# Score levels of a linear-attention mixer on two pairs of PSUM banks by turns

## Chip, cores, metric

One core of a Trainium2 chip runs the kernel. The metric is the device time of one execution in microseconds (us); the median of a few runs is compared.

## What is computed

The reference is a block of two layers of a latent generator, over 256 context tokens and 256 latent tokens with 1024 features. The even layer holds a linear-attention group with gates (GLA, 4 heads with 64 key and 128 value features) beside an mLSTM group (4 heads of 128); the odd layer is a state-space mixer. Each layer has a modulated RMSNorm ahead of it and a convolutional SwiGLU network behind it. The change touches only the scores of the GLA group. Cut to what matters, for one direction:

```
cum = jnp.cumsum(lac, axis=1)
rel = jnp.where(tri, cum[:, :, None] - cum[:, None, :], -jnp.inf)
att = jnp.einsum('bthk,bshk,btshk->bhts', qc, kc, jnp.exp(rel))
o = jnp.einsum('bhts,bshv->bthv', att, vc) + jnp.einsum('bthk,bhkv->bthv', qc * jnp.exp(cum), s)
```

The decay differs for every feature, so the score of two tokens is not a product of one matrix with another. Forward and backward scans are added up.

## The kernel before

Activations are feature-major: features on the 128 partitions, the 512 tokens along the free axis. Weights stream in as blocks of 128x128; each is split into a high and a low float32r part (`wh` by ScalarE, L168; `wl` by VectorE or GpSimd, L169), and a projection takes three products per block (L180 to L182 where features come out on partitions, L215 to L217 where tokens do). A projection of one column tile over all tokens is 24 matmuls of 512 columns.

The GLA part runs in `even_mixer`, in a loop over two pairs of heads (`for j in range(2)`); the two heads of a pair lie in the two halves of the partitions (64 each). Scores are computed by levels. A first level, without decays, gives the diagonal. Then level n, for n from 0 to 7, gives the scores between the two halves of each block of 2^(n+1) tokens: q and k are multiplied by exponentials of the cumulative gates relative to the middle of the block (tile `EX` of tag `b4`: four subtractions on VectorE, L623 to L626, an exponential on ScalarE, L627, a product on VectorE, L628), and `scores` multiplies them. In `scores`, each token tile t and head `par` gives one matmul of 64 rows by 128 columns (L597), which the profile shows as two records; a level is 8 matmuls and 16 records, and the lines are called with the two heads by turns. Head 0 writes one PSUM bank, head 1 another. Then VectorE takes each bank into `att` under the mask of the level (L603; L606 for the first level), and for level 7 ScalarE copies it into `off` (L633). The tile with `att` and `off` (tag `ao`) exists once, so head pair 1 can write it when head pair 0's outputs (L672) are through.

PSUM has eight banks: four of tag `g` (`gps`), three of tag `m` (`mps`), one of tag `v` (`vps`). Projections take tag `g`. Scores, transposes and outputs take tag `m`. A tile is asked for where the program calls it, and its bank comes free after the last reader.

In head pair 1, each level n is preceded by one of the eight projections with convolution of the mLSTM queries and keys (`ml_in.pop(0)()`, through `conv_silu`): 24 matmuls into a bank of tag `g`, then an activation on ScalarE (L571) and two taps on VectorE (L336, L337) that read the bank, and two passes more. After level 7 of head pair 1 the mLSTM values are projected (`gemm_t`, L635: four banks of tag `g`, L215 to L217).

The order of instructions is not written out by hand. The Tile scheduler lays the whole program out: each engine gets a fixed list of instructions, made by a priority that follows the program's order among what the scheduler takes to be ready, with the tiles' slots (PSUM banks, SBUF tiles by tag) given out as it goes. Each engine then works through its own list and waits on semaphores.

Of the kernel before, what the change touches and what calls it, by code (L numbers as in the profile page):

```python
# [13 lines left out]
ALU = mybir.AluOpType  # L14
AX = mybir.AxisListType

P = 128
# [6 lines left out]
# causal pieces of a 256-token segment, keys in tile t: (direction, t, queries from, to, mask column, offset)  # L24
# [27 lines left out]
def block_kernel(ctx: ExitStack, tc: tile.TileContext, A: dict, out: bass.AP):  # L52
# [55 lines left out]
    def rsqrt(ss, scale, eps):  # L108
        """(ss * scale + eps) ** -0.5 of a few columns, by Newton steps from the exponent's halving"""
        n = ss.shape[-1]  # L110
        m, y, w = (np_.tile([P, 16], F32, tag=t, name=nm(t), bufs=2)[:, :n] for t in ("rm", "ry", "rw"))
        v.tensor_scalar(out=m, in0=ss, scalar1=scale, scalar2=eps, op0=ALU.mult, op1=ALU.add)
        v.tensor_scalar(out=w.bitcast(I32), in0=m.bitcast(I32), scalar1=1, scalar2=None, op0=ALU.logical_shift_right)
        v.tensor_scalar(out=y.bitcast(I32), in0=w.bitcast(I32), scalar1=-1.0, scalar2=1597463007.0, op0=ALU.mult, op1=ALU.add)
        for _ in range(3):
            v.tensor_tensor(out=w, in0=y, in1=y, op=ALU.mult)
            v.scalar_tensor_tensor(out=w, in0=w, scalar=-0.5, in1=m, op0=ALU.mult, op1=ALU.mult)
            v.scalar_tensor_tensor(out=y, in0=w, scalar=1.5, in1=y, op0=ALU.add, op1=ALU.mult)
        return y

    def colsum(sq, c=0, ps=None):
        """column sums of sq [128, n] with the columns on partitions: [128, n / 128] of a PSUM tile"""
        nt = sq.shape[-1] // P
        ps = vps() if ps is None else ps
        for t in range(nt):
            # each product overwrites all but the first column of the one before
            te.matmul(out=ps[:, c + t:c + t + P], lhsT=sq[:, t * P:(t + 1) * P], rhs=ones[:, :P], start=True, stop=True)
        return ps[:, c:c + nt]

    def spread(col, out):  # L130
        """out[:, t] = col[t % 128, t // 128] on every partition"""
# [7 lines left out]
    class Stream:  # L139
        def __init__(self, src, nblocks, fill=None, every=1, skip=0, ahead=1, pool=rawp, eng=lambda u: v):  # L140
            """fill: other work, one piece of it put ahead of every `every`-th transfer's products;
            ahead: how many splits run ahead of the products; eng: what computes the low parts"""
# [5 lines left out]
        def load(self, d):  # L148
            """transfer d to its place in SBUF"""
            if self.rawi != d:  # L150
                w = min(16, self.n - d * 16) * P
                self.raw = self.pool.tile([P, 2048], F32, tag="raw", name=nm("raw"))
                # the first transfer in halves, its second one with its split
# [30 lines left out]
    def gemm_f(st, b0, nk, acts, c0=0, c1=T, bank=gps, ks=None):  # L184
        """feature-major: [128 columns of W, tokens c0:c1]"""
# [7 lines left out]
    def gemm_k(st, b0, nk, acts, spans, pss=None, ks=None):  # L193
        """as gemm_f for a few column tiles at once (blocks [k][tile]), so that products start with the first k"""
# [12 lines left out]
    def gemm_t(st, b0, nk, acts, tiles):  # L207
        """token-major: [128 tokens, 512 columns of W] per token tile"""
# [21 lines left out]
    def mod_chunk(l, j, pool=rawp, psa=vps, tag="raw", n=2, bufs=None):  # L230
        """512 of the vectors' columns, their weights in n transfers"""
# [11 lines left out]
    def mod_part(q, pool, psa):  # L243
        """as mod_chunk, 256 columns of the first layer's mixer norm"""
# [8 lines left out]
    def mod_out(l, c, n, ps, psa):  # L253
        """add up the quadrants, with the columns on partitions: n tiles of 128 columns from tile c"""
# [10 lines left out]
        if i in (1, 4):  # L265
            # (1 + scale) * gain, in place of scale
            v.scalar_tensor_tensor(out=dst, in0=dst, scalar=1.0, in1=col("nmg" if i == 1 else "nfg", l * 8 + k), op0=ALU.add, op1=ALU.mult)
# [3 lines left out]
    class Norm:  # L271
        """1 / rms over the features of tokens c0:c1, a feature tile at a time"""
# [17 lines left out]
        def cols(self):  # L290
            """[token % 128, token tile]"""
            return rsqrt(self.most, 1.0 / D, EPS)

        def row(self):
            """on all partitions, the tokens along the free axis"""
# [29 lines left out]
    # residual: x += gate * y  # L325
# [6 lines left out]
    def conv_side(y, ps, w0, w2):  # L332
        """the two outer taps of a width-3 convolution within each segment"""
# [12 lines left out]
    def warm(n, rhs):  # L346
        """products of ones, so that the tensor engine keeps its clock up while the first data come"""
# [3 lines left out]
    with tc.tile_pool(name="stp", bufs=6) as stp:  # L351
# [13 lines left out]
        def start(k, acts):  # L365
            # the first products run as their K tiles come, between the parts of shift and scale
# [35 lines left out]
    with ExitStack() as st:  # L402
# [6 lines left out]
        def turn(k):  # L409
            """the gain, then token-major"""  # L410
# [29 lines left out]
def even_mixer(E, st, acts, pss0, then):  # L440
# [52 lines left out]
    # log_sigmoid(x) = min(x, 0) - ln(1 + exp(-|x|)), each table loaded once  # L493
# [60 lines left out]
    # token-major columns: [t, tile, row of RQ], and the end-state weights of the context  # L554
# [30 lines left out]
    for j in range(2):  # L585
# [5 lines left out]
        def scores(Q, K, sink, flip=0):  # L591
            pps = [mps().rearrange("p (a b) -> p a b", b=P) for _ in range(2)]
# [13 lines left out]
        scores(q, k, lambda par, pp: v.scalar_tensor_tensor(out=att[par], in0=pp, scalar=2.0, in1=idb, op0=ALU.mult, op1=ALU.mult))  # L606
        for n in range(8):
# [6 lines left out]
            if n == 0:  # L614
# [3 lines left out]
                scores(EX[:, 0, :], k, masked(0))  # L618
# [11 lines left out]
            if n < 7:  # L630
                scores(Q, K, masked(n))
            else:
                scores(Q, K, lambda par, pp: s.copy(out=off[par], in_=pp), 1)  # L633
# [3 lines left out]
        # end state of the context, both directions  # L637
# [22 lines left out]
        # outputs, token-major, and their norm per head  # L660
# [28 lines left out]
    # q and k carry a factor 2 each from the tanh form of silu  # L689
# [4 lines left out]
    def head(h):  # L694
# [5 lines left out]
        # end state of the context: [k, value | norm] per direction  # L700
# [15 lines left out]
        for sg in range(2):  # L716
# [4 lines left out]
            # [s, t] weights: forward s0 -> t 0:256, s1 -> t 128:256; backward s0 -> t 0:128, s1 -> t 0:256  # L721
# [28 lines left out]
    def finish(h):  # L750
        # output gate (twice it), norm, transposed
# [53 lines left out]
def conv_ffn(E, st, l, acts, fill, then):  # L805
# [20 lines left out]
    def around(y, ps, ti):  # L826
        """the other taps"""
# [15 lines left out]
    # VectorE keeps to one operand from SBUF where GpSimd works beside it  # L843
# [3 lines left out]
    def project(j):  # L847
# [5 lines left out]
        elif not full:  # L853
            # a pair to a bank; the others hold sums of the down-projection
# [3 lines left out]
        else:  # L858
            # the down-projection takes the usual banks before the last two are through
# [9 lines left out]
    for hf in range(nh):  # L869
# [6 lines left out]
        for jj in range(per):  # L876
# [4 lines left out]
            # the down-projection's first columns, as far as their K tiles are there  # L881
# [4 lines left out]
            if jj == per - 2 and not full:  # L886
                # and a column more while the last pairs are convolved
# [25 lines left out]
        if full and last:  # L913
            # the last two a segment at a time, so that the next norm starts on the first
# [6 lines left out]
def odd_mixer(E, st, acts, then):  # L921
# [13 lines left out]
    # dt, B, C, B: the context first, C without it  # L935
# [8 lines left out]
    def conv_silu(b0, ti, out, c0):  # L944
        """out = 2 silu(conv + bias)"""
# [13 lines left out]
    def group(q):  # L959
# [5 lines left out]
        # x and B each carry a factor 2  # L965
# [6 lines left out]
        # [s, dir, 384]: forward s0 x t 0:256, s1 x t 128:256; backward s1 x t 0:256, s0 x t 0:128  # L972
# [12 lines left out]
    # softplus(x) = max(x, 0) + ln(1 + u), u = exp(-|x|), with the rounding of 1 + u put back  # L985
# [24 lines left out]
    # token-major: context w_end = exp(c_end - cum) dt [s, dir*32 + head]; latent cum and dt  # L1010
# [7 lines left out]
    tok = T_([P, 2, P], "tokc")     # [s, tile, cum (64) | dt (64)]  # L1018
# [33 lines left out]
    def tokens(i):  # L1052
        """token-major x: context weighted for the end state, latent by dt, per direction; D x"""
# [4 lines left out]
        xw = T_([P, 2, 2, 2, 64], "xw", pool=sp)    # [s, tile, dir, head, 64]  # L1058
        xd = T_([P, 2, 2, 2, 64], "xd", pool=sp)    # [s, dir, tile, head, 64]
# [13 lines left out]
    def decays(i):  # L1073
        """masked C B^T times the decays between tokens; the cumulative sums (negated) broadcast to all partitions"""
# [3 lines left out]
        G = T_([P, 2, 2, 384], "G", pool=sp)        # [s, dir, head, parts]  # L1078
# [15 lines left out]
    def inter(i):  # L1094
        """from the end states, each direction, times its decay since them"""
# [9 lines left out]
    def outputs(i):  # L1105
# [9 lines left out]
        # times (twice) silu(z), square sum per group  # L1115
# [41 lines left out]
def blocks_f(w, ms):  # L1157
    """feature-major blocks of w (K, M): for each column tile, its K tiles"""
# [3 lines left out]
def blocks_k(w, ms):  # L1162
    """feature-major blocks, for each K tile its column tiles"""
# [3 lines left out]
def blocks_kf(w):  # L1167
    """four column tiles together, then the other four one by one"""
# [3 lines left out]
def blocks_t(w, c0):  # L1172
    """token-major blocks: for each K tile, four column tiles from c0"""
# [11 lines left out]
def cols(vv):  # L1185
    """vector -> [128, n] with feature f at [f % 128, f // 128]"""
# [3 lines left out]
def layout(inp):  # L1190
# [40 lines left out]
    # even in-projection  # L1231
# [19 lines left out]
    # FFN  # L1251
# [11 lines left out]
    # odd in-projection  # L1263
# [12 lines left out]
    # constants of the shapes  # L1276
# [29 lines left out]
```

## Time and profile before

| | |
|---|---|
| runs | 1298.69, 1298.11, 1303.0 us; median 1298.69 |
| span of the profiled execution, first to last instruction | 1300.7 us |
| TensorE (PE) busy | 1245.6 us, 96% |
| VectorE (DVE) busy | 942.7 us, 72% |
| ScalarE (ACT) busy | 597.2 us, 46% |
| GpSimd (POOL) busy | 381.4 us, 29% |
| mean granted clock of TensorE | 0.989 |

The profile gives one execution; of its own time only the span is known, which lies between the second and the third of the runs. Times in rows are counted from the span's start. Busy time is the union of an engine's instructions; matmuls overlap in the array, so their single durations add up to more than it. The clock is a share of full speed: 1.00 is 2.4 GHz and 0.50 is 1.2 GHz.

### The profile page before, as it was taken

The numbers are of one execution on the slowest core, as the hardware profiler recorded it, in microseconds if no ns is written. First come the engines' busy times: TensorE is split into PE (matmuls) and PEld (weight loads), VectorE is DVE, ScalarE is ACT, GpSimd is POOL, SyncE is SP. The second block draws the span as 40 slices with busy tenths as digits, with TensorE's granted clock in tenths as the row PEclk, the third lists the DMA queues.
The fourth block names the chain that finished last, engine by engine and source line by source line (L and its number), as shares of the span: only waits on it lengthen the run. The fifth ranks groups of instructions, "written<-read, shape, count | busy, mean of one in ns | idle before, by whom it ended". The sixth has DMA issues, their size and how long they took to land.

```text
span 1300.7 us, 19329 instructions
## 1 busy us (share of the span) xinstructions
PE 1245.6 (96%) x7358; PEld 1027.8 (79%) x7358; DVE 942.7 (72%) x2137; ACT 597.2 (46%) x947; POOL 381.4 (29%) x214
## 2 busy tenths in 40 slices
PE   7999999999999999999999998999999999899987
PEld 5557787876867777888888897888888888899987
DVE  4483899576659766237774488788888957999993
ACT  3463344343344433124442266565566545555553
POOL 0100000000226646136664000122222124678720
PEclk8999999999999999999999999999999998999999
DMA  9556303324445664232202136444363473545431
GB/s 373 184 190 230 117 12 111 109 89 165 166 175 213 254 232 135 98 123 97 98 33 98 65 106 175 130 153 131 114 152 105 153 251 132 207 164 181 156 130 66
DMA packets 39964, 190.96 MB, mean 147 GB/s; under 512 B 4592, under 2 KB 10552, under 8 KB 20928
## 3 DMA queue, kind: packets, MB, share of 16 engines
q1 hardware_dynamic: 36512, 185.48, 41.3%
q10 hardware_dynamic: 3360, 4.25, 1.1%
q8 instruction: 58, 0.95, 0.3%
q14 instruction: 34, 0.28, 0.1%
HBM read 188.51 MB, written 1.20 MB: 146 GB/s over the span
## 4 chain that ended last, share of the span: by engine, by line
PE 71%; DVE 19%; ACT 3%; issue 3%; DMA 3%; POOL 1%; SPq 0%; ACTq 0%; DVEq 0%; POOLq 0%
PE gps L180 14%; PE gps L181 13%; PE gps L182 13%; DVE y L829 6%; PE mps L180 4%; PE mps L182 4%; PE mps L181 4%; PE vps L239 3%; PE vps L1114 2%; DVE ml L897 2%; DVE y L893 1%; PE gps L215 1%; PE gps L217 1%; PE gps L216 1%; PE vps L1100 1%
## 5 line engine op out<-in xcount | busy, mean ns | idle before, releaser
L169 POOL TENSOR_TENSOR wl<-raw,wh 128x1024 fp32r<-128x1024 f32 x111 | 268.1, 2426 | 515.2 <-ACT wh L168 515.0
L168 ACT ACTIVATE wh<-raw 128x1024 fp32r<-128x1024 f32 x226 | 237.3, 1054 | 173.1 <-PE gps L182 107.3
L180 PE MATMUL gps<-hh,wh 128*128 128x512 f32 (+1 forms) x840 | 297.1, 355 | 7.1 <-ACT hh L316 5.4
L182 PE MATMUL gps<-hl,wh 128*128 128x512 f32 (+1 forms) x840 | 295.6, 354 | 1.6 <-DVE hl L318 1.6
L181 PE MATMUL gps<-hh,wl 128*128 128x512 f32 (+1 forms) x840 | 295.4, 352 | 0.4 <-DVE wl L169 0.3
L829 DVE SCALAR_TENSOR_TENSOR y<-mps,fcw,y 128x255 f32<-128x255 f32 (+3 forms) x576 | 223.0, 426 | 38.7 <-ACT y L823 32.5
L169 DVE TENSOR_TENSOR wl<-raw,wh 128x1024 fp32r<-128x1024 f32 x115 | 140.9, 1232 | 81.1 <-ACT wh L168 80.9
L180 PEld LDWEIGHTS gps<-hh,wh 128*128 128x128 f32 x840 | 159.5, 190 | 43.2 <-issue 12.1
L180 PE MATMUL mps<-hh,wh 128*128 128x256 f32 (+1 forms) x528 | 172.7, 327 | 10.9 <-DVE y L829 8.6
L182 PEld LDWEIGHTS gps<-hl,wh 128*128 128x128 f32 x840 | 160.0, 191 | 25.0 <-issue 4.2
L181 PEld LDWEIGHTS gps<-hh,wl 128*128 128x128 f32 x840 | 160.0, 191 | 23.6 <-issue 4.1
L181 PE MATMUL mps<-hh,wl 128*128 128x256 f32 (+1 forms) x528 | 171.1, 324 | 0.0
L182 PE MATMUL mps<-hl,wh 128*128 128x256 f32 (+1 forms) x528 | 171.1, 324 | 0.0
L180 PEld LDWEIGHTS mps<-hh,wh 128*128 128x128 f32 x528 | 101.0, 191 | 27.8 <-issue 9.3
L180 PE MATMUL gps<-mh,wh 128*128 128x256 f32 (+1 forms) x352 | 117.7, 334 | 2.7 <-ACT mh L896 2.7
L181 PE MATMUL gps<-mh,wl 128*128 128x256 f32 (+1 forms) x352 | 117.2, 333 | 0.0
L182 PE MATMUL gps<-ml,wh 128*128 128x256 f32 (+1 forms) x352 | 117.0, 333 | 0.0
L182 PEld LDWEIGHTS mps<-hl,wh 128*128 128x128 f32 x528 | 101.1, 192 | 7.4
L181 PEld LDWEIGHTS mps<-hh,wl 128*128 128x128 f32 x528 | 101.0, 191 | 7.3
L829 DVE SCALAR_TENSOR_TENSOR y<-gps,fcw,y 128x189 f32<-128x189 f32 (+3 forms) x196 | 83.2, 437 | 23.3 <-ACT y L823 19.4
L823 ACT ACTIVATE y<-mps,fcw 128x256 f32<-128x256 f32 (+1 forms) x66 | 40.6, 639 | 87.7 <-PE mps L182 87.7
L180 PEld LDWEIGHTS gps<-mh,wh 128*128 128x128 f32 x352 | 66.8, 190 | 10.0 <-ACT mh L896 2.9
(281 smaller groups left out, 1850.4 us busy)
## 6 DMA issues: line engine op xcount, KB each, us to landing
raw<-in_up SPq DMA_DIRECT2D x42, 1024.0 KB, 5.0
rawm<-in_modw SPq DMA_DIRECT2D x36, 1024.0 KB, 5.7
raw<-in_win SPq DMA_DIRECT2D x32, 1024.0 KB, 5.4
raw<-in_dn SPq DMA_DIRECT2D x20, 1024.0 KB, 5.0
raw<-in_wout SPq DMA_DIRECT2D x10, 1024.0 KB, 5.1
rawm<-in_mods SPq DMA_DIRECT2D x8, 1024.0 KB, 14.0
R<-crd SPq DMA_DIRECT2D x32, 256.0 KB, 4.5
rawm<-in_modw SPq DMA_DIRECT2D x8, 512.0 KB, 5.3
```

What stands on the lines that cost most here:

```text
L168: s.activation(out=hi[:, :n], in_=rw, func=AF.Copy)
L169: self.eng(u).tensor_tensor(out=lo[:, :n], in0=rw, in1=hi[:, :n].bitcast(F32), op=ALU.subtract)
L180: te.matmul(out=ps, lhsT=lhi, rhs=rhi, start=first, stop=False)
L181: te.matmul(out=ps, lhsT=llo, rhs=rhi, start=False, stop=False)
L182: te.matmul(out=ps, lhsT=lhi, rhs=rlo, start=False, stop=last)
L215: te.matmul(out=ps, lhsT=ah[:, sl], rhs=hi[:, c:c + 512], start=k == 0, stop=False)
L216: te.matmul(out=ps, lhsT=ah[:, sl], rhs=lo[:, c:c + 512], start=False, stop=False)
L239: te.matmul(out=ps[32 * (k % 4):32 * (k % 4) + 32, :], lhsT=spad[:, k, :], rhs=raw[:, kk * 512:(kk + 1) * 512], start=k < 4, stop=k >= 4)
L823: s.activation(out=y, in_=ps, func=AF.Identity, scale=fcw[:, ti * 10 + 4:ti * 10 + 5], bias=fcw[:, ti * 10 + 9:ti * 10 + 10])
L829: v.scalar_tensor_tensor(out=o, in0=i, scalar=fcw[:, ti * 10 + wi:ti * 10 + wi + 1], in1=o, op0=ALU.mult, op1=ALU.add)
L897: part = lambda ya=ya, h_=h_, l_=l_: ep.tensor_tensor(out=l_, in0=ya, in1=h_.bitcast(F32), op=ALU.subtract)
L1114: te.matmul(out=py[r, a:e], lhsT=l, rhs=rr, start=n == 0, stop=n == len(mm) - 1)
```

## The change

`scores` gets the number of the level and takes its two banks from tag `m` for an even number and from tag `g` for an odd one. The first level is called with 1. In a head pair the levels then ask for `g`, `m`, `g`, `m`, and so on, to `g` for level 7. Matmuls, masks and their order in the program stay the same. The rest of the diff takes comments and docstrings out.

```
-        def scores(Q, K, sink, flip=0):
-            pps = [mps().rearrange("p (a b) -> p a b", b=P) for _ in range(2)]
+        def scores(n, Q, K, sink, flip=0):
+
+            pps = [(mps, E.gps)[n % 2]().rearrange("p (a b) -> p a b", b=P) for _ in range(2)]
...
-        scores(q, k, lambda par, pp: v.scalar_tensor_tensor(out=att[par], in0=pp, scalar=2.0, in1=idb, op0=ALU.mult, op1=ALU.mult))
+        scores(1, q, k, lambda par, pp: v.scalar_tensor_tensor(out=att[par], in0=pp, scalar=2.0, in1=idb, op0=ALU.mult, op1=ALU.mult))
...
-                scores(EX[:, 0, :], k, masked(0))
+                scores(0, EX[:, 0, :], k, masked(0))
...
-                scores(Q, K, masked(n))
+                scores(n, Q, K, masked(n))
...
-                scores(Q, K, lambda par, pp: s.copy(out=off[par], in_=pp), 1)
+                scores(n, Q, K, lambda par, pp: s.copy(out=off[par], in_=pp), 1)
```

## Rows read from the trace of the kernel before

**Rows 1.** The page, part 1: busy time, share and instructions of each engine.

```profile
PE 1245.6 (96%) x7358; PEld 1027.8 (79%) x7358; DVE 942.7 (72%) x2137; ACT 597.2 (46%) x947; POOL 381.4 (29%) x214
```

**Rows 2.** Windows: stretch, length, busy time of each engine, clock, DMA.

```profile
139.70:158.50 18.80, 18.17 (x115) 14.42 (x111) 18.75 (x34) 7.31 (x7) 0.00 (x0) 1.00 0.30 112
158.50:222.70 64.20, 62.74 (x393) 51.12 (x393) 58.60 (x117) 30.74 (x43) 0.00 (x0) 1.00 0.15 51
222.70:238.90 16.20, 16.17 (x83) 13.42 (x84) 5.81 (x6) 4.96 (x7) 0.00 (x0) 1.00 0.38 127
238.90:330.00 91.10, 88.15 (x485) 67.58 (x484) 67.08 (x243) 36.81 (x78) 0.00 (x0) 1.00 0.42 139
```

**Rows 3.** Windows, TensorE's instructions on tag g alone: busy (count), clock, DMA.

```profile
139.70:158.50 18.80, 11.47 (x47) 1.00 0.30 112
...
213.70:222.70 9.00, 7.51 (x32) 1.00 0.38 126
```

**Rows 4.** Timeline of TensorE, score records: start, length, instruction, idle before.

```profile
144.14 2.37 PE L597 MATMUL mps<-b 64*128 64x128 f32 x16 [0.31 <-DVE b L628]
...
158.51 1.16 PE L597 MATMUL mps<-b 64*128 64x128 f32 x16
```

**Rows 5.** Windows, TensorE's instructions of L597 alone.

```profile
131.40:137.90 6.50, 6.18 (x64) 1.00 0.24 102
180.80:186.10 5.30, 4.89 (x48) 1.00 0.01 3
```

**Rows 6.** Timeline of VectorE within head pair 0.

```profile
138.40 1.35 DVE L603 COPY_PREDICATED ao<-lev,mps 128x512 f32<-128x512 int8 x2
...
150.32 1.21 DVE L628 TENSOR_TENSOR b<-b,qk 128x1024 f32<-128x1024 f32 x1
...
156.78 1.22 DVE L628 TENSOR_TENSOR b<-b,qk 128x1024 f32<-128x1024 f32 x1
```

**Rows 7.** Instructions on tile ce: durations, first and last start.

```profile
L640 DVE TENSOR_SCALAR ce<-cum x2: 133/137/141, 95.8 to 97.0; 128x1 f32<-128x1 f32 x2
```

**Rows 8.** Timeline of ScalarE.

```profile
67.35 0.56 ACT L473 COPY qk<-gps 128x512 f32<-128x512 f32 x1
...
130.90 0.60 ACT L549 ACTIVATE t<-gps 128x512 f32<-128x512 f32 x1 [3.77 <-PE gps L182]
...
132.01 0.53 ACT L644 ACTIVATE t<-cum,ce 128x256 f32<-128x256 f32 x1
```

**Rows 9.** Timeline of TensorE: projections and the first level of head pair 1.

```profile
139.74 0.50 PE L180 MATMUL gps<-hh,wh 128*128 128x512 f32 x1
...
172.54 0.39 PE L180 MATMUL gps<-hh,wh 128*128 128x512 f32 x1
...
180.03 0.40 PE L180 MATMUL gps<-hh,wh 128*128 128x512 f32 x1
...
180.80 1.51 PE L597 MATMUL mps<-qk 64*128 64x128 f32 x13
```

**Rows 10.** The chain that ended last, at level 7 of head pair 1.

```profile
221.45 1.15 DVE b L628
222.73 1.16 PE mps L597 x16
```

**Rows 11.** Groups by line, 100 to 260 us: count, busy, mean ns, idle before.

```profile
L571 ACT ACTIVATE t<-gps,c 128x512 f32<-128x512 f32 x8 | 6.2, 769 | 0.4 <-PE gps L182 0.4
L336 DVE SCALAR_TENSOR_TENSOR t<-gps,c,t 128x510 f32<-128x510 f32 x8 | 5.9, 739 | 0.0
```

**Rows 12.** Timeline of TensorE around an empty stretch.

```profile
84.17 0.39 PE L217 MATMUL gps<-wh,hl 128*128 128x512 f32 x1
87.81 1.94 PE L239 MATMUL vps<-rawm,spad 128*32 128x512 f32 x8 [3.25 <-DVE mod L263]
```

**Rows 13.** Windows behind that stretch.

```profile
87.80:91.10 3.30, 3.29 (x11) 1.36 (x12) 3.30 (x5) 2.03 (x4) 0.00 (x0) 0.50 0.20 34
91.50:96.00 4.50, 4.50 (x24) 3.41 (x26) 4.50 (x12) 2.13 (x2) 0.00 (x0) 1.00 0.89 340
```

## Prediction

> **What bounds the kernel now.** I read the page first: TensorE is busy for 96% of the span [rows 1], so time is won by taking work from it and lost by leaving it without any. Then the windows around the stage that is changed, 131 to 239 us [rows 2]: TensorE is busy for 18.17 of 18.80 us while head pair 0 is scored, 62.74 of 64.20 us through head pair 1, and 16.17 of 16.20 us in what follows. VectorE is full in the first of these (18.75 of 18.80) and near full in the second (58.60 of 64.20). So two engines are full together, and the reader should ask what keeps TensorE full: the chain level, mask, next level runs through VectorE, and the scores alone do not fill TensorE. The same window for bank tag `g` alone answers it: between 139.7 and 158.5 us TensorE runs 47 projection matmuls, 11.47 of the 18.80 us [rows 3]. They belong to the mLSTM convolutions, which the program calls later, within head pair 1; they are run ahead into the holes of head pair 0. The same happens at 213.7 to 222.7 us: 32 matmuls on tag `g`, nearly all of the value projection L635, run ahead of the last level.
>
> The timeline of TensorE comes next [rows 4]. A level is 16 records. Where the two heads alternate it lasts 1.16 us (158.51), where one head comes whole and then the other 2.37 us (144.14). So 1.2 us is the most that one level can give.
>
> **The change: what it gives.** Nine of the 18 levels do not alternate: the first four of pair 0, the first three of pair 1, and two single ones in pair 0, the earlier of them at 144.14. The three of pair 1 hold 5.3 us with 48 records [rows 5]; three times 1.16 is 3.5, so 1.8 us can be had. The four of pair 0 hold 6.5 us with 64 records [rows 5]; 4.65 would do, 1.9 us. The two single ones give 1.2 each. All of it is 6.1 us, 0.47% of the span, and this is the upper bound of the gain. In pair 0 (4.3 us of it) VectorE is the full engine [rows 2], and level 7 at 158.51 waits for its product L628 (156.78 to 158.00) [rows 6], not for the scores before it. I count pair 0 at nothing as long as TensorE has room there, and pair 1 at its 1.8 us.
>
> The edit adds no instruction: 288 records of L597 before and after, the same masks, no DMA. What it moves is which banks are asked for. The first level and levels 1, 3, 5, 7 of each pair now ask for two banks of tag `g`, which has four and which the projections use.
>
> **What it takes.** How are banks given out? Two places of the trace say: in the order in which the program calls for tiles of a tag, and a tile is not given out before the one called before it has its first writer placed. First, the exponentials of L644 need `ce`, written at 95.8 to 97.0 us, and cumulative sums that are older [rows 7]; ScalarE is idle for 3.77 us before 130.90, yet L644 runs at 132.01, after the L549 of 130.90, which writes the tile of tag `t2` called before it [rows 8]. That tag has six slots, and each tile of L549 is done with after the next step, so slots were free. Second, pair 1's first level is called before the convolutions' projections, and its q and k are there since 67.9 us (L473 at 67.35, 0.56 long) [rows 8]. When the masks of 138.40 are through at 139.75, no score bank is in use [rows 6], and TensorE takes the projection at 139.74, not that level, which runs at 180.80 [rows 9]. With banks to whoever is ready it would have been the other way round; in program order pair 0's later score, transpose and output tiles of tag `m` come first.
>
> By that order the program's list for tag `g` after the change is: pair 0's first level, 1, 3, 5, 7; pair 1's first level; projections 0 and 1; level 1; projections 2 and 3; level 3; and so on; level 7; the value projection's four. Projection 0 can then not start before level 7 of pair 0 is placed, at 158.5, and the value projection not before level 7 of pair 1.
>
> Step by step, from level 7 of pair 0 (158.51) to the end of the value projection (238.9), a stretch of 80.4 us in which TensorE is full [rows 2]:
>
> The 47 matmuls lose their place before it. Their pitch is 0.227 us, (180.03 - 172.54) / 33 [rows 9]. 47 x 0.227 = 10.7 us. From below this would be 0, if other products filled the holes; I find none in the program that is called early enough and has its inputs, so I take 10.7.
>
> The three levels of pair 1: -1.8 us.
>
> The 32 matmuls of 213.7 to 222.7: they are work that stays in the stretch, so they cost nothing while TensorE has the displaced 47 in their place: 32 x 0.227 = 7.3 us goes out ahead of level 7 and 10.7 comes in, and level 7 comes at 222.73 - 7.3 + 10.7 - 1.8 = 224.3 or later. VectorE, when full, had its product for that level ready at 222.6 [rows 10]. The two are within 2 us of each other, so neither has much cover. Projections now also alternate with score levels for the four banks, and a projection's bank is free only after a ScalarE pass and two convolution taps on VectorE (0.77 and twice 0.74 us [rows 11]). Bounds of what this leaves empty: 0, and 7.3 us, if TensorE got nothing in place of the hoisted value projection. I take 2 us, nearer to the lower end, because projection k+1 (24 x 0.227 = 5.4 us) covers the 2.2 us of projection k's release.
>
> The clock. Between the levels of pair 0 TensorE will be empty. Level 6 starts when its product is through (150.32 + 1.21) and lasts 1.16, to 152.7; level 7 has its product at 158.0 [rows 6]: 5.3 us. Before level 5 there is a hole much like it. The trace has such a hole: last product at 84.17, next at 87.81, and then 3.3 us at a granted clock of 0.50 (1.2 GHz), at 1.00 again from 91.5 [rows 12, 13]. Half of 3.3 is 1.65 us lost in each. The first falls into pair 0, where TensorE has room; the second falls on level 7 and what follows, and counts: 1.7 us. Bounds: 0 and 3.3, for both.
>
> The Trainium skill ("TensorE: Matmul & The Clock Gate", part 1) advises for models that the ramp is under 1% of a typical kernel and a count of slow matmuls should not be fitted; by it this term would be left out and the sum be 10.9. I keep the row, since it shows that very hole. The skill's "TensorEngine Tiling (Array Packing)", gotcha 1, warns that row tiling raises the pressure on PSUM banks; it has no price for it.
>
> Sum: 10.7 - 1.8 + 2 + 1.7 = +12.6 us. The stretch after, to 330 us, has TensorE busy for 88.15 of 91.10 [rows 2], so the delay passes on. The profiled execution would go from 1300.7 to 1313.3; the runs' median lies 2.0 below its span, so 1298.7 + 12.6 = **1311 us**.
>
> **Rivals.** A: banks go to whoever is ready, or the projections keep their holes in another way. Then nothing is displaced, and the gain is between pair 1's 1.8 and all 6.1 us: 1293 to 1297, say **1296**, not slower. For it: no row shows the order of banks for tag `g` itself, whose tiles have so far been asked for by projections alone. Against it: the two places above, of tags `t2` and `m`. It decides if projection 0 starts before 150 us. Chance 0.14.
>
> B: the displaced work is mostly swallowed. VectorE is the bound of pair 1, TensorE's share there is partly waiting that the profile shows as busy, and only what VectorE loses counts: half of 10.7 less 1.8 gives +3.6, **1302**. For it: VectorE's 58.60 of 64.20. Against it: matmuls follow each other at 0.227 us there, which is no waiting. Chance 0.12.
>
> C: lockstep. TensorE and VectorE wait for each other through the four banks in each of the four rounds, and the whole 7.3 us of the value projection are lost too, with both clock terms: 10.7 - 1.8 + 7.3 + 3.3 = +19.5, **1318**. Chance 0.10.
>
> **Chances and range.** The likeliest case has 0.64, C 0.10, B 0.12, A 0.14. A measurement of this kernel can tell about 0.5%, 6.5 us. The likeliest case stays under 6.5 us only if the terms at their lower ends meet (8.9), so nearly all of it and all of C are slower: 0.72. B and most of A are the same: 0.24. A beyond its bound: 0.04. The likeliest case's own range is 1307 to 1316. The range from 1298 to 1319 holds B, C and the slower edge of A.
>
> **What would show it.** In the profile after: no projection matmul on tag `g` between 138 and 158 us, and some 10 us of empty TensorE there, with a clock of 0.5 around 158 to 162; pair 1's first level right after level 7 of pair 0, near 160 instead of 180.8; every level 1.16 us at full clock, with its heads alternating; the value projection's first product behind level 7 of pair 1, its last near 251 instead of 238.8; masks and products on VectorE unchanged in number and length. I am wrong if projection 0 still starts near 140 us (A), if level 7 of pair 1 comes no later than 223 us with the stretch's end within 4 us of before (B), or if TensorE's holes between 160 and 240 us add up to more than 6 us (C).

## The result and the profile after

Five runs of the changed kernel have a median of 1307.66 us (1306.1 to 1312.11), five of the kernel before 1298.69 us (1297.91 to 1303.0). The ratio is 1.0058, interval 1.0041 to 1.0074: slower by about 7.5 us. (The two medians alone lie 9.0 us apart; losses and gains of runs are worked out from the ratios below.) The forecast was 1311 us, +12.6, within 1298 to 1319. Sign, place and cause hold; the size was put 5 us too high.

The lines below are the page of the changed kernel, part 1, and its windows (columns as in [rows 2]). All lines from 597 on stand one higher than before: scores are L598, the masks L604, the product L629.

```profile
PE 1242.4 (95%) x7358; PEld 1025.5 (79%) x7358; DVE 943.5 (72%) x2137; ACT 597.9 (46%) x947; POOL 381.4 (29%) x214
```

```profile
139.70:158.50 18.80, 9.97 (x76) 8.61 (x77) 17.61 (x31) 6.86 (x7) 0.00 (x0) 0.73 0.23 97
158.50:180.00 21.50, 20.85 (x148) 17.86 (x147) 16.71 (x51) 7.78 (x12) 0.00 (x0) 1.00 0.00 1
180.00:222.70 42.70, 42.70 (x251) 34.08 (x249) 40.39 (x63) 19.22 (x23) 0.00 (x0) 1.00 0.24 79
222.70:246.50 23.80, 23.50 (x114) 18.97 (x113) 8.20 (x9) 9.46 (x15) 0.00 (x0) 1.00 0.23 81
```

The instruction counts are those of [rows 1]; TensorE even has 3.2 us less busy time, 2.5 of it in the score records of both pairs (28.1 us before, 25.6 after, by the groups from 131 to 235 us). Yet the kernel is longer, so TensorE is idle longer. The first window shows where: 9.97 us busy of 18.80, where [rows 2] had 18.17. Who has left shows in the groups by line of that window, all of TensorE's that there are:

```profile
L598 PE MATMUL mps<-b 64*128 64x128 f32 x32 | 4.1, 430 | 3.0 <-DVE b L629 3.0
L598 PE MATMUL gps<-b 64*128 64x128 f32 x32 | 3.3, 365 | 6.5 <-DVE b L629 6.5
L658 PE MATMUL mps<-tok,t 128*128 128x256 f32 x8 | 2.0, 392 | 0.7 <-ACT t L654 0.7
L652 PE MATMUL mps<-c,t 128*128 128x128 f32 x4 | 1.1, 435 | 0.0
```

No projection is left there, against 47 of their matmuls in [rows 3]. The last column says what TensorE waits for instead: 9.5 us for VectorE's product of the next level. The timeline of TensorE (columns as in [rows 4]) follows the stage through:

```profile
142.07 1.87 PE L598 MATMUL gps<-b 64*128 64x128 f32 x16 [3.83 <-DVE b L629]
...
148.40 1.41 PE L598 MATMUL gps<-b 64*128 64x128 f32 x16 [2.69 <-DVE b L629]
...
152.85 2.08 PE L598 MATMUL mps<-b 64*128 64x128 f32 x16 [3.04 <-DVE b L629]
154.86 1.12 PE L652 MATMUL mps<-c,t 128*128 128x128 f32 x4
156.71 1.99 PE L658 MATMUL mps<-tok,t 128*128 128x256 f32 x8 [0.73 <-ACT t L654]
...
158.85 1.16 PE L598 MATMUL gps<-b 64*128 64x128 f32 x16
160.36 0.49 PE L598 MATMUL gps<-qk 64*128 64x128 f32 x4
...
168.68 0.48 PE L180 MATMUL gps<-hh,wh 128*128 128x512 f32 x1
...
182.36 1.16 PE L598 MATMUL gps<-b 64*128 64x128 f32 x16
...
222.92 1.16 PE L598 MATMUL gps<-b 64*128 64x128 f32 x16
224.01 0.50 PE L215 MATMUL gps<-wh,hh 128*128 128x512 f32 x1
```

Level 7 of pair 0 comes at 158.85, 0.34 us later than in [rows 4]. Pair 1's first level begins at 160.36, not at 180.80 [rows 9]. Projection 0 begins only at 168.68, where [rows 9] had it at 139.74. The value projection starts behind level 7 of pair 1 and runs on with one gap, of 0.30 us. TensorE's next other work is a transpose at 246.51, 7.8 us later than in the kernel before. These are the lines of it, of before and of after:

```profile
238.73 0.60 PE L651 MATMUL mps<-c,t 128*128 128x128 f32 x4
```

```profile
225.28 0.50 PE L215 MATMUL gps<-wh,hh 128*128 128x512 f32 x1 [0.30 <-ACT ao L634]
...
246.51 0.60 PE L652 MATMUL mps<-c,t 128*128 128x128 f32 x4
```

At the last copy out of the value projection, on ScalarE, after is also 7.8 us behind before, at 330 us 7.4, at 760 us 7.1, and at the end of the span (1305.9 against 1300.7) 5.2. Most of the last step is no gain of the change: between 1075 and 1090 us the granted clock of the profiled execution of before falls twice (0.74 and 0.71 in two windows of 5 us), that of after once (0.66).

### The profile page after: what moved, and what is told of

It reads as the page before. It is cut to its first block, busy times and chain, and to the rows that moved or that the text cites. A ratio compares the mean times of both kernels' runs of the same rounds, so it can differ in the third digit from the quotient of the medians.

```text
span 1305.9 us, 19322 instructions
## 1 busy us (share of the span) xinstructions
PE 1242.4 (95%) x7358; PEld 1025.5 (79%) x7358; DVE 943.5 (72%) x2137; ACT 597.9 (46%) x947; POOL 381.4 (29%) x214
## 4 chain that ended last, share of the span: by engine, by line
PE 74%; DVE 16%; ACT 4%; issue 3%; DMA 2%; POOL 1%; SPq 0%; ACTq 0%; DVEq 0%; POOLq 0%
PE gps L180 14%; PE gps L182 14%; PE gps L181 14%; DVE y L830 6%; PE mps L180 4%; PE mps L182 4%; PE mps L181 4%; PE vps L239 3%; PE vps L1115 2%; DVE ml L898 2%; PE gps L215 1%; PE gps L216 1%; PE gps L217 1%; DVE y L894 1%; PE vps L1101 1%
## 5 line engine op out<-in xcount | busy, mean ns | idle before, releaser
L180 PE MATMUL gps<-hh,wh 128*128 128x512 f32 (+1 forms) x840 | 297.2, 355 | 7.1 <-ACT hh L316 5.4
L182 PE MATMUL gps<-hl,wh 128*128 128x512 f32 (+1 forms) x840 | 295.3, 353 | 1.6 <-DVE hl L318 1.6
L181 PE MATMUL gps<-hh,wl 128*128 128x512 f32 (+1 forms) x840 | 294.8, 351 | 0.3 <-DVE wl L169 0.3
L180 PEld LDWEIGHTS gps<-hh,wh 128*128 128x128 f32 x840 | 159.6, 190 | 42.4 <-issue 11.3
L180 PE MATMUL mps<-hh,wh 128*128 128x256 f32 (+1 forms) x528 | 172.0, 326 | 10.8 <-DVE y L830 8.5
L182 PEld LDWEIGHTS gps<-hl,wh 128*128 128x128 f32 x840 | 159.9, 191 | 25.1 <-issue 4.2
L181 PEld LDWEIGHTS gps<-hh,wl 128*128 128x128 f32 x840 | 160.1, 191 | 22.8 <-issue 4.1
L181 PE MATMUL mps<-hh,wl 128*128 128x256 f32 (+1 forms) x528 | 170.6, 323 | 0.0
L182 PE MATMUL mps<-hl,wh 128*128 128x256 f32 (+1 forms) x528 | 170.5, 323 | 0.0
L180 PEld LDWEIGHTS mps<-hh,wh 128*128 128x128 f32 x528 | 100.3, 190 | 27.6 <-issue 9.3
L180 PE MATMUL gps<-mh,wh 128*128 128x256 f32 (+1 forms) x352 | 117.6, 334 | 2.7 <-ACT mh L897 2.7
L181 PE MATMUL gps<-mh,wl 128*128 128x256 f32 (+1 forms) x352 | 117.1, 333 | 0.0
L182 PE MATMUL gps<-ml,wh 128*128 128x256 f32 (+1 forms) x352 | 116.9, 333 | 0.0
L182 PEld LDWEIGHTS mps<-hl,wh 128*128 128x128 f32 x528 | 100.4, 190 | 7.4
L181 PEld LDWEIGHTS mps<-hh,wl 128*128 128x128 f32 x528 | 100.4, 190 | 7.3
L180 PEld LDWEIGHTS gps<-mh,wh 128*128 128x128 f32 x352 | 66.9, 190 | 10.0 <-ACT mh L897 2.9
```

Of the source, the lines that this page charges most:

```text
L180: te.matmul(out=ps, lhsT=lhi, rhs=rhi, start=first, stop=False)
L181: te.matmul(out=ps, lhsT=llo, rhs=rhi, start=False, stop=False)
L182: te.matmul(out=ps, lhsT=lhi, rhs=rlo, start=False, stop=last)
```

## The experiments

Twelve kernels were run; each ratio is against runs of the kernel before beside it, whose median lay at 1301 to 1303 us. The line that most of them edit is called the bank line.

**One pair alone, and the first levels alone.** Three edits of the bank line:

```
-pps = [(mps, E.gps)[n % 2]() ...
+pps = [(mps, E.gps)[n % 2 if j == 0 else 0]() ...     # pair0_only
+pps = [(mps, E.gps)[n % 2 if j == 1 else 0]() ...     # pair1_only
+pps = [(mps, E.gps)[j == 0 and n == 1]() ...          # first_levels
```

> Only head pair 0 takes banks by turns; pair 1 has its old ones. Theory (banks of a tag go out in the program's order, so the projections lose their place in the holes of pair 0): the hole at 139.7 to 158.5 us stays as in the changed kernel, no projection in it, and the time is 5 to 9 us over the kernel before. Rival (four banks are too few where projections and levels take turns in pair 1): no loss, -2 to +2 us.

> Only head pair 1 takes banks by turns. Theory: pair 1's first level is scored within the holes of pair 0 and then holds two of the four banks until its sink at about 169 us; projections 0 and 1 keep their place, but projection 2 is now called behind level 1 of pair 1 and can't run ahead, so TensorE has a hole from about 168 to 175 us: +1 to +6 us. Rival (only the hole of pair 0 costs time): the better alternation in pair 1 shows, -2 to 0 us.

> Only the first level and level 1 of pair 0 take banks of tag g, ahead of every projection in the list. Theory: no projection is displaced, the first four levels alternate in some 5 us instead of 6.5, and VectorE, which is full behind them, hides it: -2 to +0.5 us. Rival (scores on tag g cost time wherever they are): +2 us or more.

pair0_only took 1311.24 us, ratio 1.0067 (1.0042 to 1.0093): pair 0's part alone has the whole loss. TensorE is busy for 8.78 us of the window 139.7 to 158.5 (9.97 in the changed kernel). first_levels took 1301.33 us, 0.9996 (0.9982 to 1.0009): the first four levels last 5.0 us instead of the 6.5 of [rows 5], the projections keep their place, and nothing comes of it. So what is gained in pair 0 is hidden behind VectorE.

pair1_only took 1309.74 us, 1.0064 (1.0046 to 1.0082), more than was expected of it (+8.3 us, against +1 to +6). These are lines of its timeline of TensorE, and its windows:

```profile
137.64 0.27 PE L598 MATMUL gps<-qk 64*128 64x128 f32 x1
...
179.27 1.11 PE L685 MATMUL mps<-c,b 128*128 128x128 f32 x4 [7.63 <-DVE b L679]
...
182.88 1.96 PE L598 MATMUL gps<-b 64*128 64x128 f32 x13
184.77 0.55 PE L180 MATMUL gps<-hh,wh 128*128 128x512 f32 x1
```

```profile
139.70:158.50 18.80, 17.24 (x115) 13.04 (x107) 18.30 (x33) 7.30 (x7) 0.00 (x0) 1.00 0.29 112
...
170.00:179.30 9.30, 1.10 (x9) 0.89 (x9) 9.29 (x30) 5.44 (x9) 0.00 (x0) 0.75 0.00 0
179.30:222.70 43.40, 43.40 (x254) 35.35 (x255) 42.30 (x68) 17.92 (x21) 0.00 (x0) 0.94 0.14 49
```

Pair 0's holes are filled here. Pair 1's first level is on tag `g`, first in its list, and is scored in the middle of pair 0 (137.64, operand `qk`). The next hole opens at 170 us: projection 2 is called after pair 1's level 1, which now has tag `g` too, and begins at 184.77, right behind that level's records (operands `gps<-b`, from 182.88). This is the same displacement in another place. The last row tells what came on top: from 179.3 us on TensorE is full, at a mean clock of 0.94, so the low rate left over from the hole takes some 0.06 x 43.4 = 2.6 us there (an estimate from this row). The two parts don't add up (8.7 and 8.3 us for one alone, 7.5 for both). That fits projections which are displaced once, whichever level holds them up first.

**One single level.** The bank line with `[j == 0 and n == 7]`: level 7 of pair 0 alone takes tag `g`.

> One single level takes banks of tag g: level 7 of pair 0. All others have their old banks and alternate as before or worse. Theory (order of calls): one call of that tag late in pair 0 is enough to keep the projections behind it, so the hole of pair 0 and the loss are those of pair0_only: +6 to +10 us. Rival (the loss grows with the number of levels that take banks from the projections): a fifth of it or less, 0 to +2 us.

It took 1310.69 us, 1.0073 (1.0048 to 1.0097). These are its groups by line in the window 139.7 to 158.5, all of TensorE's, and its timeline around level 7:

```profile
L598 PE MATMUL mps<-b 64*128 64x128 f32 x64 | 8.3, 386 | 8.0 <-DVE b L629 8.0
L658 PE MATMUL mps<-tok,t 128*128 128x256 f32 x6 | 2.9, 658 | 0.7 <-ACT t L654 0.7
L652 PE MATMUL mps<-c,t 128*128 128x128 f32 x4 | 1.1, 436 | 0.0
```

```profile
155.92 3.78 PE L658 MATMUL mps<-tok,t 128*128 128x256 f32 x8 [0.73 <-ACT t L654]
...
160.06 1.16 PE L598 MATMUL gps<-b 64*128 64x128 f32 x16
161.15 0.49 PE L673 MATMUL mps<-tok,ao 128*128 128x128 f32 x2
161.39 0.48 PE L180 MATMUL gps<-hh,wh 128*128 128x512 f32 x1
```

This is the plainest of the runs. Two of the four banks of tag `g` are asked for by no score there, the same number that the two projections of [rows 3] fill, and still no projection runs in that window. The first one comes 0.24 us after the first product that follows level 7. It isn't a lack of banks that holds it up, but the place of its call in the list of tag `g`. On this run's trace pair 1's transpose (L652) begins at 246.42, 7.7 us later than before, so one level has the whole loss of the changed kernel (7.8 on its trace). The 9.5 us of the ratio have an interval of 6 to 13.

**The same banks, the projections called earlier.** Before, the first two projections are called in pair 1. Here they are called in pieces between the levels of pair 0, into a bank each; `conv_silu` then takes that bank.

```
+pieces = {2: ((104, 0, 4),), 4: ((104, 4, 8), (112, 0, 2)), 6: ((112, 2, 8),)}
...
-ps = E.gemm_f(W, b0, KD, acts)
+ps = early[b0] if b0 in early else E.gemm_f(W, b0, KD, acts)
...
 scores(n, Q, K, masked(n))
+if j == 0:
+    for p in pieces.get(n, ()):
+        piece(*p)
```

It was run with the banks of pair0_only, of the changed kernel and of the kernel before.

> As pair0_only with the same banks, but projections 0 and 1 are called in pieces within pair 0, behind levels 2, 4 and 6, while their convolutions stay where they were. Theory: only the order of calls kept the projections out, so 40 to 48 of their matmuls are back before 160 us and the loss of pair0_only goes: -4 to +2 us against the kernel before. Rival (too few banks): the loss stays, +4 us or more.

> The changed kernel's banks for both pairs, with projections 0 and 1 called in pieces within pair 0 as in pair0_called_early. Theory: the hole of pair 0 is filled, but projection 2 is still called behind level 1 of pair 1, whose first level holds the other two banks until about 168 us; the hole moves to 165 to 178 us, as in pair1_only: +4 to +9 us. Rival (pair 0's hole is the whole loss): -4 to +1 us.

> The kernel before (all scores on tag m) with the calls of pair0_called_early. Theory: alternation in pair 0 is hidden behind VectorE, so what pair0_called_early gained over the kernel before comes from the calls: -4 to -1 us, within 1 us of it. Rival (its gain was the alternation of pair 0): -1 to +1.5 us.

With pair 0's banks it took 1298.91 us, 0.9979 (0.9964 to 0.9994), which is faster than both kernels (2.7 us under the kernel before). It differs from pair0_only by the order of calls alone, and 11 us lie between the two ratios. Its groups by line and window (scores are L607 there):

```profile
L180 PE MATMUL gps<-hh,wh 128*128 128x512 f32 x14 | 5.8, 413 | 0.0
...
L607 PE MATMUL gps<-b 64*128 64x128 f32 x48 | 3.5, 285 | 0.0
```

```profile
139.70:158.50 18.80, 16.67 (x130) 13.16 (x130) 18.76 (x33) 9.53 (x14) 0.00 (x0) 1.00 0.19 80
```

Three times 14 projection matmuls are back (L181 and L182 have as many), scores use the same tag beside them, and the clock is at 1.00. A rival by which four banks are too few for both falls with this.

With the banks of the changed kernel it took 1309.95 us, 1.0059 (1.0042 to 1.0075). Its windows show pair 0's hole gone and pair 1's, that of pair1_only, in its place:

```profile
139.70:158.50 18.80, 16.93 (x131) 13.31 (x132) 18.76 (x32) 9.54 (x14) 0.00 (x0) 1.00 0.17 69
170.00:180.00 10.00, 2.77 (x12) 2.18 (x13) 10.00 (x30) 3.48 (x5) 0.00 (x0) 0.52 0.00 0
```

With the banks of before it took 1300.68 us, 0.9989 (0.9975 to 1.0002). This can't be told from 0.9979, so it stays open whether the 2.7 us of the best version are owed to the banks at all, or to the earlier calls.

**The two projections convolved early, too.** In addition, the first two `ml_in.pop(0)()` are called in pair 0 behind its levels, with pair 0's new banks and with those of before.

```
-if j == 1:
+if j == 1 and ml_in:
     ml_in.pop(0)()
...
+if j == 0:
+    ml_in.pop(0)()
+    ml_in.pop(0)()
 pt = mps()...
```

> As pair0_called_early, and the convolutions of projections 0 and 1 are called in pair 0 too, behind its KE and QI, so that VectorE has them in the stretch from 158 to 170 us where it is half idle, and later projections move up one place or two. Theory: VectorE and TensorE are both full in pair 1, so work moved ahead is won: -7 to -3 us against the kernel before. Rival (pair 0's outputs are held up by it): -2 us or slower.

> As called_and_convolved_early with all scores on their old banks. Theory: the gain is of the calls, not of the banks: within 1.5 us of called_and_convolved_early. Rival (banks by turns in pair 0 give the gain once the holes are filled): 2 us or more slower than it.

1303.0 us, 1.0017 (0.9999 to 1.0035), and 1305.27 us, 1.0021 (1.0006 to 1.0036): the gain that was expected isn't there, the first can't be told from the kernel before, the second is slower by 2.7 us, and the banks make no difference. Two levels of pair 1 now have no projection ahead of them, and TensorE is busy for 41.26 and 41.27 us of 180 to 222.7, 1.4 us short of full in both; the first also has a clock of 0.92 there. But the kernel before has 41.61 there, so the holes explain little of it, and why the gain of the earlier calls is gone stays open.

**The order of the records.** `for par in range(2)` goes outside `for t in range(4)`, so that one head comes whole before the other; on the banks of before, and on those of the changed kernel.

> The kernel before, with the two loops of a level exchanged: all four tiles of one head, then of the other, so that no level alternates. Theory: alternation is worth 1.2 us a level where TensorE is the bound (levels 2 to 7 of pair 1, six of them) and little in pair 0, where VectorE is: +3 to +7 us. Rival (the levels' order in the array is hidden everywhere): -1 to +1 us.

> The changed kernel with the same exchange: the banks by turns, but no level alternates. Theory: the loss of the changed kernel (+7.5) and 1.2 us for each of pair 1's eight or nine levels on top, as TensorE is full there: +14 to +20 us against the kernel before. Rival (alternation is hidden): +6 to +9 us.

On the old banks it took 1302.84 us, 1.0012 (0.9997 to 1.0027), which isn't the loss that was expected. A level on its timeline of TensorE:

```profile
186.93 1.68 PE L598 MATMUL mps<-b 64*128 64x128 f32 x16
```

So at full clock heads by turns are worth 0.52 us per level (1.68 - 1.16), where [rows 4] suggested 1.2. One head alone takes 1.16 us for its 8 records; the second head of pair 1's level 1 in the kernel before shows it:

```profile
185.00 1.16 PE L597 MATMUL mps<-b 64*128 64x128 f32 x8 [0.41 <-DVE ao L603]
```

Two heads without any overlap would take twice that, 2.3 us, which is about the 2.37 of [rows 4]. That wasn't the price of the program's order but of a wait within the level: the trace of before has 0.3 us there for the mask L603 of the level before, which still reads a bank, so the second head couldn't begin while the first ran.

On the new banks it took 1315.73 us, 1.0092 (1.0065 to 1.0119), between the two expectations. Against the 1.0058 of the changed kernel this is 4 us more, but it can't be put down to the 18 levels. The profiled execution, the slowest of six (1306.54 to 1318.01 us), has a low clock behind the hole:

```profile
158.50:170.00 11.50, 11.50 (x57) 10.01 (x57) 1.81 (x3) 2.23 (x4) 0.00 (x0) 0.58 0.00 0
```

TensorE is full there, so the low rate alone takes some 0.42 x 11.5 = 4.8 us of this execution (an estimate from the row).

**The hole kept busy.** Products of ones, 256 columns wide, go into the score banks ahead of levels 3 to 7 of pair 0, and the scores overwrite them. This added work is to hold the clock up, so that its price shows.

```
+for i in range({3: 12, 4: 2, 5: 16, 6: 2, 7: 16}.get(n, 0) if j == 0 and Q is not q else 0):
+    te.matmul(out=pps[i % 2]...[:, :256], lhsT=ones[:, :P], rhs=ones, start=True, stop=True)
```

> The changed kernel, with products of ones put into the banks of levels 3 to 7 of pair 0 ahead of the scores, which overwrite them; they fill the hole but compute nothing that is kept. Theory: the half clock inside the hole (0.73 on average there) costs only what it adds to the levels on the way to level 7, about 1 us, and nothing after 158 us; with the clock held at 1.00 the time is -2 to +1.5 us of the changed kernel, that is +5 to +9 us against the kernel before. Rival (the clock is a large part of the loss): +3 us or less against the kernel before.

It took 1316.99 us, 1.0131 (1.0108 to 1.0154). The timeline of TensorE tells why it can't serve (scores are L600):

```profile
152.85 7.17 PE L595 MATMUL gps<-ones 128*128 128x256 f32 x32
159.95 1.16 PE L600 MATMUL gps<-b 64*128 64x128 f32 x16
```

Sixteen products last 7.17 us, longer than the 5.3 us that the prediction gave the hole, and level 7 comes 1.1 us later than after. And what had moved into the hole of the changed kernel is out of it again: pair 0's transposes and end state begin at 161.05 and 162.76, behind level 7, and 16 records of another stage (L239, 1.92 us), which run there at 136.32, come at 171.77. The value projection ends at 252.47, 6.0 us later than after. The clock did stay at 1.00, but neither expectation is met (+17 us), and the run doesn't tell what the clock costs.

## Why the prediction was right, and where its size was off

"In the order in which the program calls for tiles of a tag": this holds, and level7_of_pair0_only with pair0_called_early shows it: a score level on tag `g` holds back each projection called after it, and an earlier call brings it back. Rival A falls. It was read off tags `t2` and `m`, a reading that carried over to tag `g`.

"47 matmuls lose their place: 10.7 us": from 158.8 us to the end of the value projection the changed kernel runs 192 matmuls of L180 to L182, before ran 145 from level 7 to the same point. That is 47 more, as forecast, at the pitch of before. Counted up to the start of the next record, waits apart, they take 45.2 us against 35.0: 10.2 us more.

"I find none in the program" to fill the holes: this step failed. Pair 0's own transposes (L652) and end state (L658) moved ahead of level 7, to 154.86 and 156.71; before (L651 and L657) they lay behind it:

```profile
159.61 0.66 PE L651 MATMUL mps<-c,t 128*128 128x128 f32 x4
...
161.32 1.99 PE L657 MATMUL mps<-tok,t 128*128 128x256 f32 x8
```

They don't depend on the scores and are called on tag `m`. They take 0.41 + 1.83 us out of the stretch by their starts: 2.2 us back. Two products of the outputs (L673, from 158.54) moved ahead as well, but the 46 records left behind level 7 take 5.5 us, where the 48 of before took 5.3: +0.2.

"The three levels of pair 1: -1.8 us": -0.3. Pair 1's first level comes in three pieces between pair 0's outputs (0.49, 0.71 and 0.49 us on the timeline), level 0 takes 2.02 and only level 1 the 1.16 us. By starts these are 4.6 us instead of 4.9; the 5.3 of [rows 5] hold a wait of 0.41 us besides, which counts with the idle time of the next term.

"What this leaves empty: 2 us": TensorE loses 0.3 us to the four banks, the gap at 225.28, where ScalarE still copies level 7 out of its two. In all it is idle for 0.65 + 0.30 us between 158.5 and 246.5, and was for 1.46 + 0.03 between 158.5 and 238.9 [rows 2]: -0.5. Rival C named over 6 us as its sign and falls. One projection lies between each two levels and covers both the level's chain and the release of a bank.

"The clock: 1.7 us": 0 in the profiled execution. The clock fell inside the hole, where it cost little: 0.73 in the first window above, and four levels there (3 to 6) last 1.41 to 2.08 us instead of 1.16. It was back before level 7:

```profile
152.80:155.00 2.20, 2.15 (x17) 1.96 (x18) 2.20 (x4) 1.06 (x1) 0.00 (x0) 0.50 0.00 0
155.00:158.50 3.50, 2.77 (x12) 2.19 (x13) 2.46 (x4) 0.59 (x1) 0.00 (x0) 0.86 0.00 0
```

Level 6 ran at the lower rate, the end state took 1.99 us as before, and from 158.5 us on the clock is 1.00. That this term came out as 0 is partly luck. In level7_of_pair0_only the low rate lasted longer (a clock of 0.59 in 139.7 to 158.5 us, against 0.73), and the same end state, just ahead of level 7, took 3.78 us at a clock of 0.50 (155.9 to 159.7 us): 1.8 us more than at 1.00, about the size that was forecast. No run isolates the term, and the five executions of the changed kernel (mean clock 0.983 to 0.987) have one profile between them.

The sum: 10.2 - 2.2 + 0.2 - 0.3 - 0.5 = 7.4 us. Measured on the trace, from level 7 of pair 0 to the transpose behind the value projection: 246.51 - 158.85 = 87.66 us, against 238.73 - 158.51 = 80.22 before, so +7.4; with the 0.34 us by which level 7 itself is late it is the 7.8 us of TensorE's delay, near the 7.5 of the ratio. So the forecast was 5 us too high on balance: it left out the work that fills the hole (2.2), and put the empty time (2.5), the clock (1.7) and the projections (0.5) too high. The gain in pair 1's levels was put too high as well, by 1.5 us, which makes up for a part of it.

The signs named ahead came out in part. No projection is left in the hole, and pair 1's first level begins at 160.36. But the clock is not low behind 158 us, level 0 of pair 1 takes 2.02 us, and level 7 of pair 1 comes at 222.92, not at 224.3 or later. That is the first half of rival B's sign; the second, an end within 4 us of before, fails.

Rival B (+3.6) assumed that VectorE's load swallows half of the displaced work; VectorE is less busy than before in that stretch (16.71 + 40.39 = 57.10 of 64.20 us against 58.60), and 180 to 222.7 us, where TensorE has 42.70 of 42.70, has no room for it. It falls.

The upper bound of the gain, 6.1 us, counted each single level at 1.2 us. By heads_in_turn_old_banks 0.52 us of that is the alternation; the rest went with the wait for a bank. first_levels gets nothing for its 1.5 us, so what stays of the gain is the 0.3 us of pair 1.

## What to carry to other kernels

Before work is moved onto another tag, list who asks for that tag after it and fills a hole now: a tile doesn't overtake an earlier call of its own tag, and one level of 1.16 us cost as much as the whole change by holding back projections behind it (level7_of_pair0_only: 9.5 us by the ratio, 7.7 on its trace). If banks have to be shared, call the filling work where the hole is (pair0_called_early: 11 us better than the same banks without it). And when counting what is displaced, look in the stages on the other tags, too, for what may move into the hole. Ask as well whether the low clock of a hole lasts beyond it: in the hole it costs little, behind it TensorE pays (some 2.6 us in pair1_only).

## What the runs showed of the hardware that was not expected

One head's 8 score records alone take 1.16 us, both heads by turns take 1.16 us as well, and one head called behind the other 1.68 us, all at full clock: in that order, too, the two overlap in part. Products of ones with 256 columns at full rows took 7.17 us for 16 instructions (32 records, 0.22 us a record), while a projection matmul of 512 columns has a pitch of 0.227 us [rows 9]: float32 operands on the one side, the split float32r parts on the other.
